# The MLP's second product as seven block products, with the token combinations made in its first

## The chip, the cores and the metric

The kernel runs on one core of a Trainium2 chip. A core has five engines that each work through a queue of their own, in order: TensorE (PE) multiplies, VectorE (DVE), ScalarE (ACT) and GpSimd (POOL) work element by element, and SyncE (SP) issues the transfers between memory and the core's SBUF. Products are added up in PSUM, which the other engines read. The metric is the time of one execution on the device in microseconds; a lower number is better. The kernel before takes 3046.49 us, the median of three runs (3045.34 to 3056.3). Everything runs in fp32, and a product in fp32 is made of three matmuls: each operand is split into a rounded part "hi" and a remainder "lo", and hi·hi, lo·hi and hi·lo are added.

## The reference

One decoder layer on 2048 tokens of width 1024: two kinds of attention, a cross-attention, and an MLP. The change touches the last step of the MLP and what the step before it leaves behind:

```python
    u = rms_norm(x, g_mlp[l]) @ w_up[l]
    x = x + jnp.square(jax.nn.relu(u)) @ w_down[l]
return rms_norm(x, g_final)
```

`w_up` is 1024 x 4096 and `w_down` 4096 x 1024.

## The kernel before

The tile framework orders the work when the kernel is built: its scheduler lays down one queue for each engine, with a wait at an instruction that needs another engine's result or a buffer that is still in use. At run time an engine goes through its queue in order. Buffers come from pools: 36 "main" tiles of 4 KB per partition, 6 "stage" tiles for what is loaded, smaller "work" tiles, and PSUM banks s (four), t (two) and o (two).

`phase_up` makes u = relu(x·w_up)². It takes the tokens in two halves of 1024, and in each half the 4096 columns in 16 pairs of 256. A pair is a 2 x 2 block matrix of weights times a 2 x 2 block matrix of tokens, and it uses seven block products in place of eight (Winograd's form): `product` (L1085 to L1097) splits one weight block or sum of blocks (ACT at L1088, POOL or DVE at L1089) and issues 84 matmuls in a pair. The sums of weights s1 to s4 are made on POOL (L1080 to L1083). The token combinations t1 to t4 stand ready in SBUF as operands: `mlp_combine` (L1009 to L1042) makes those of half 1 during pairs 4 to 11 of half 0 and puts them to memory, and `mlp_operands` (L1045 to L1067) loads and splits all seven when the halves change. `out` (L1102 to L1107) finishes one 128 x 512 block of u and stores it, four for each pair.

`phase_down` multiplies u by `w_down` directly. It goes over 16 slices of 256 rows of `w_down`. For a slice `slab` (L109 to L117) loads two weight tiles of 128 x 1024 and splits them (ACT at L116, POOL at L117), and for each of four chunks of 512 tokens a tile of u is loaded and split (ACT at L141, DVE at L142). Then eight output blocks of six matmuls each follow (L1179), each added by DVE into an accumulator in SBUF (L1183) that began as the residual x2: 3072 matmuls of 512 columns in all. `finish` (L1142 to L1171) makes the last norm of a chunk: squares on ACT (L1149), their sum on POOL or DVE (L1153), column sums on PE, the scale, and the store.

## Time and profile before

| | |
|---|---|
| median of three runs | 3046.49 us (3045.34 to 3056.3) |
| the profiled execution | 3047.63 us |
| its span in the trace | 3045.6 us, granted clock 0.974 of full speed |
| busy: PE / DVE / ACT / POOL | 95% / 58% / 37% / 38% |
| `phase_up` on PE | about 1665.7 to 2302.7 us |
| `phase_down` on PE | 2302.7 to 3006.4 us |
| after the last product | 39.2 us |

The profiled execution lies 1.1 us above the median, and 2.0 us of it are outside the span. "Busy" is the share of the span in which an engine executes; the chain of waits goes back from the last instruction to what released each step.

### The profile page before, as it was taken

How to read it: one execution, taken by the hardware profiler on the slowest of the kernel's cores; microseconds unless marked ns; L12 is line 12 of the kernel's file. 1: busy time of each engine (PE TensorE's matmuls, PEld its weight loads, DVE VectorE, ACT ScalarE, POOL GpSimd, SP SyncE). 2: the span in 40 equal slices, each digit the busy share in tenths (PEclk: the TensorE clock that was granted, in tenths of full speed). 3: DMA queues.
4: the chain of work that ended last, by engine and by line, in shares of the span. 5: the costliest groups of instructions: out<-in, count | busy, mean ns of one | idle time of the engine just before them, and what ended most of it. 6: DMA issues, size and time to landing. Idle time of an engine off the chain costs nothing.

```text
span 3045.6 us, 38727 instructions
## 1 busy us (share of the span) xinstructions
PE 2884.5 (95%) x13740; PEld 2350.0 (77%) x13740; DVE 1760.0 (58%) x2918; ACT 1125.9 (37%) x2481; POOL 1163.8 (38%) x914
## 2 busy tenths in 40 slices
PE   8999989989999899999995999989999999999996
PEld 8978866666666688888883877878888888888886
DVE  5254448887788642423345756665556566656656
ACT  7221137666767422444223333433342111111113
POOL 0133336765676542112124666665561101110115
PEclk9999989989999999999997999999999999999997
DMA  8443363434432664211327345443346122212203
GB/s 310 133 178 126 111 197 115 121 84 140 126 109 81 196 208 138 84 42 66 108 90 276 124 148 170 145 154 111 111 139 228 63 76 77 77 63 77 77 7 111
DMA packets 223297, 380.21 MB, mean 125 GB/s; under 512 B 25313, under 2 KB 95105, under 8 KB 223105
## 3 DMA queue, kind: packets, MB, share of 16 engines
q1 hardware_dynamic: 223104, 377.75, 37.5%
q8 instruction: 108, 1.77, 0.2%
q14 instruction: 85, 0.69, 0.1%
HBM read 259.65 MB, written 116.98 MB: 124 GB/s over the span
## 4 chain that ended last, share of the span: by engine, by line
PE 61%; DVE 5%; DMA 4%; POOL 4%; issue 2%; ACT 1%; SPq 0%; POOLq 0%; DVEq 0%; ACTq 0%
PE pd L1179 23%; PE p L1093 15%; PE po L804 6%; PE sc L868 6%; PE po L992 5%; PE sc L482 1%; DMA xs<-x_d 1%; DVE p L528 1%; PE o L543 1%; POOL w L1089 1%; PE wo L659 1%; DMA wf<-w_up 1%; PE pv L934 1%; PE pq L828 1%; POOL p L521 1%
## 5 line engine op out<-in xcount | busy, mean ns | idle before, releaser
L1093 PE MATMUL p<-xh,w 128*128 128x512 f32 x1792 | 557.3, 392 | 42.9 <-ACT w L1088 27.6
L1183 DVE TENSOR_TENSOR acc<-pd,acc 128x512 f32<-128x512 f32 (+1 forms) x520 | 351.2, 681 | 253.7 <-PE pd L1179 251.2
L1093 PEld LDWEIGHTS p<-xh,w 128*128 128x128 f32 x1792 | 337.0, 189 | 121.3 <-ACT w L1088 29.6
L1179 PE MATMUL pd<-uh,wdh 128*128 128x512 f32 (+1 forms) x1040 | 401.7, 386 | 1.0 <-DVE acc L1183 1.0
L1179 PE MATMUL pd<-ul,wdh 128*128 128x512 f32 (+1 forms) x1040 | 401.2, 386 | 0.0
L1179 PE MATMUL pd<-uh,wdl 128*128 128x512 f32 (+1 forms) x1040 | 401.2, 386 | 0.0
L1093 PE MATMUL p<-xl,w 128*128 128x512 f32 x896 | 350.3, 391 | 0.0
L117 POOL TENSOR_TENSOR wdl<-wf,wdh 128x1024 fp32r<-128x1024 f32 x32 | 78.0, 2440 | 549.6 <-ACT wdh L116 543.8
L489 ACT ACTIVATE p<-sc,nm 128x512 f32<-128x512 f32 (+3 forms) x320 | 198.8, 627 | 95.9 <-DVE nm L488 94.3
L482 PE MATMUL sc<-kt,q 128*128 128x512 f32 (+2 forms) x640 | 199.1, 414 | 32.0 <-ACT p L489 22.4
L1179 PEld LDWEIGHTS pd<-uh,wdh 128*128 128x128 f32 x1040 | 195.3, 188 | 40.4 <-DVE acc L1183 1.2
L1179 PEld LDWEIGHTS pd<-ul,wdh 128*128 128x128 f32 x1040 | 195.3, 188 | 39.4
L1179 PEld LDWEIGHTS pd<-uh,wdl 128*128 128x128 f32 x1040 | 195.3, 188 | 39.3
L488 DVE TENSOR_REDUCE nm<-sc 128x1 f32<-128x512 f32 (+3 forms) x320 | 184.3, 601 | 51.5 <-PE sc L487 29.4
L1093 PEld LDWEIGHTS p<-xl,w 128*128 128x128 f32 x896 | 169.1, 189 | 35.2
L482 PEld LDWEIGHTS sc<-kt,q 128*128 128x128 f32 x640 | 108.7, 199 | 84.4 <-ACT p L489 43.4
L521 POOL TENSOR_TENSOR p<-p,scl 128x512 f32<-128x512 f32 (+3 forms) x144 | 151.6, 1081 | 55.0 <-DVE scl L516 50.2
L141 ACT CAST uh<-uf 128x1024 fp32r<-128x1024 f32 x64 | 65.8, 1049 | 276.2 <-PE pd L1179 263.7
L303 PE MATMUL pa<-hh,wh 128*128 128x512 f32 x416 | 162.7, 391 | 0.0
L303 PE MATMUL pa<-hl,wh 128*128 128x512 f32 x416 | 162.5, 391 | 0.0
L303 PE MATMUL pa<-hh,wl 128*128 128x512 f32 x416 | 162.1, 390 | 0.0
L172 POOL TENSOR_TENSOR tot<-tot,sq 128x512 f32<-128x512 f32 x56 | 77.5, 1384 | 207.8 <-ACT sq L171 206.1
(266 smaller groups left out, 6051.8 us busy)
## 6 DMA issues: line engine op xcount, KB each, us to landing
wf<-w_up SPq DMA_DIRECT2D x64, 512.0 KB
u_d<-u SPq DMA_DIRECT2D x128, 256.0 KB
uf<-u_d SPq DMA_DIRECT2D x64, 512.0 KB
qk_d<-rot SPq DMA_DIRECT2D x96, 256.0 KB
x_d<-x SPq DMA_DIRECT2D x32, 512.0 KB
x<-x_d SPq DMA_DIRECT2D x32, 512.0 KB
xs<-x_d SPq DMA_DIRECT2D x32, 512.0 KB
wf<-w_down SPq DMA_DIRECT2D x32, 512.0 KB
```

What stands on the lines that cost most here:

```text
L117: getattr(nc, eng).tensor_tensor(lo, wf, f(hi), op=ALU.subtract)
L303: nc.tensor.matmul(pa, s_[d // 4][:, P * (d % 4) : P * (d % 4) + P], hs(m_, c, d), start=(d == 0 and i == 0), stop=(d == DT - 1 and i == 2),)
L482: mm = nc.tensor.matmul(sc[:, :um], q[:, x, c, P * t : P * t + P], kt[:, c, :um], start=(x == 0), stop=(x == 1 and not last))
L488: nc.vector.tensor_reduce(nm[:, t, j, c : c + 1], sc[:, :u], axis=AX.X, op=ALU.max, negate=True)
L489: nc.scalar.activation(p[:, c, :u], sc[:, :u], AF.Exp, bias=nm[:, t, j, c : c + 1], accum_out=l[:, t, j, c : c + 1])
L521: nc.gpsimd.tensor_tensor(p[:, 1, :u], p[:, 1, :u], sc[:, t, j, 1:2].broadcast_to([P, u]), op=ALU.mult)
L804: nc.tensor.matmul(po, wo[d][s_][:, P * n : P * n + P], m_[d // 2][:, d % 2], start=(d == 0 and z == 0), stop=(d == 7 and z == 2))
L868: nc.tensor.matmul(sc[n], x[s_][d][:, ts], wq[d][m_][:, 512 * n : 512 * n + 512], start=(d == 0 and z == 0), stop=(d == DT - 1 and z == 2))
L992: nc.tensor.matmul(po[i], vw[b][s_][:, P * n : P * n + P], m_[b], start=(b == 0 and z == 0), stop=(b == 7 and z == 2))
L1093: nc.tensor.matmul(ps, t[:, s_, P * d : P * d + P], x[d][m_], start=(d == 0 and z == 0), stop=(d == 3 and z == 2))
L1179: nc.tensor.matmul(pd, w[ft][s_][:, P * n : P * n + P], u[m_][:, ft, ts], start=(ft == 0 and z == 0), stop=(ft == 1 and z == 2))
L1183: nc.vector.tensor_tensor(av, pd, av, op=ALU.add)
```

## The change

The product with `w_down` takes the form of the first one. The loop is now over two halves of the tokens, four groups of 1024 rows of `w_down`, and seven products. A product has four output blocks (m) of 12 matmuls, so there are 2 x 4 x 7 x 4 x 12 = 2688 matmuls (the last product is done in two pieces of 256 columns). Seven accumulators of 512 x 512 take the place of the residual sums: in the first group of a half ACT copies the PSUM block into the accumulator (L1264), in the later ones DVE adds it (L1266). The accumulators are put together at the end of the half (`total`), and the residual is added on POOL. `weights` loads four blocks of `w_down` for a group into wide tiles, once for each half, and makes the sums in one tile `ws` on POOL and DVE (L1211). `parts` splits weights ("wd") and tokens ("ub") in two pieces of 128 x 1024 each: the cast on ACT (L1192), the lower part of the first piece on POOL and of the second on DVE (both L1193).

The token combinations are made in `phase_up`: each pair adds two subtractions on DVE and two on POOL and stores seven blocks in place of four.

```diff
-            nc.sync.dma_start(k.u_d[CHUNKS[2 * half + j]][n][i], u)
+            if (i, j) != (0, 1):
+                nc.sync.dma_start(k.u_d[half][f"b{i + 1}{j + 1}"][n], u)
+            return u
...
+        t = [k.main([P, 2, 512], F32, name="ut") for _ in range(2)]
+        t1, t2, t3, t4 = (x[:, i] for x in t for i in range(2))
+        nc.vector.tensor_tensor(t1, b12, b11, op=ALU.subtract)
+        nc.gpsimd.tensor_tensor(t2, b22, t1, op=ALU.subtract)
+        nc.gpsimd.tensor_tensor(t3, b22, b12, op=ALU.subtract)
+        nc.vector.tensor_tensor(t4, b21, t2, op=ALU.subtract)
+        for i, x in enumerate((t1, t2, t3, t4)):
+            nc.sync.dma_start(k.u_d[half][f"t{i + 1}"][n], x)
...
+    PRODUCTS = ((1, "b11"), (6, "t2"), (5, "t1"), (7, "t3"), (2, "b21"), (3, "b22"), (4, "t4"))
...
+    def parts(src, name):
+        res = []
+        for y in range(2):
+            x = src(y)
+            t = [k.main([P, 2, 512], name=name) for _ in range(2)]
+            nc.scalar.copy(t[0], x)
+            (nc.vector if y else nc.gpsimd).tensor_tensor(t[1], x, f(t[0]), op=ALU.subtract)
+            res.append(t)
+        return res
...
+        def combine(out, p, q, op):
+            for y, eng in enumerate((nc.gpsimd, nc.vector)):
+                ys = slice(2 * y, 2 * y + 2)
+                eng.tensor_tensor(out[:, ys], p[:, ys], q[:, ys], op=op)
+        yield parts(cut(a11), "wd")
+        s = wide("ws", "s", 1)
+        combine(s, a21, a22, ALU.add)
+        s1 = parts(cut(s), "wd")
+        combine(s, s, a11, ALU.subtract)
+        yield parts(cut(s), "wd")
+        yield s1
...
+                        if first:
+                            nc.scalar.copy(av, pd)
+                        else:
+                            nc.vector.tensor_tensor(av, pd, av, op=ALU.add)
...
+                if g == 3 and n == 3:
+                    ends.append(finish(acc[3] + acc[7], CHUNKS[2 * half + 1], 0, 512, False))
+                    step(-1)
```

ACT in the first group of the second product, after the change (copies of PSUM into accumulators, casts of the next product's weights "wd" and tokens "ub"):

```order
L1264 COPY acc_20394<-pd_20593 128x512
L1264 COPY acc_20394<-pd_20607 128x512
L1264 COPY acc_20395<-pd_20621 128x512
L1192 CAST wd_20651<-wa_20407 128x1024
L1192 CAST wd_20655<-wa_20407 128x1024
L1264 COPY acc_20395<-pd_20635 128x512
L1192 CAST ub_20661<-ub_20659 128x1024
L1192 CAST ub_20667<-ub_20665 128x1024
L1264 COPY acc_20396<-pd_20671 128x512
L1264 COPY acc_20396<-pd_20685 128x512
L1264 COPY acc_20397<-pd_20699 128x512
```

and the same engine early in `phase_down` before:

```order
L141 CAST uh_20556<-uf_20554 128x1024
L141 CAST uh_20626<-uf_20624 128x1024
L141 CAST uh_20696<-uf_20694 128x1024
L116 CAST wdh_20764<-wf_20766 128x1024
L116 CAST wdh_20770<-wf_20772 128x1024
L141 CAST uh_20778<-uf_20776 128x1024
L141 CAST uh_20848<-uf_20846 128x1024
```

Before, ACT had casts alone there; after, a product's fourth copy stands between the casts of the next product's weights and those of its tokens.

SP at the seam of the two products, after the change (the last pair's stores to `u_d`, then the first loads of `w_down`; "x2" at the end of a row stands for two such rows):

```order
L1108 DMA u_d1b11_110<-u_20330 128x512
L1129 DMA u_d1t1_113<-ut_20376 128x512
L1129 DMA u_d1t3_115<-ut_20377 128x512
L1129 DMA u_d1t2_114<-ut_20376 128x512
L1108 DMA u_d1b21_111<-u_20371 128x512
L1129 DMA u_d1t4_116<-ut_20377 128x512
L103 DMA wa_20404<-w_down 128x2x512 x2
L103 DMA wa_20407<-w_down 128x2x512 x2
L103 DMA wa_20410<-w_down 128x2x512 x2
L103 DMA wa_20413<-w_down 128x2x512 x2
```

and before, where SP took up `w_down` three pairs ahead of the end of `phase_up`:

```order
L1107 DMA u_d0_12_115<-u_19624 128x512
L1107 DMA u_d1_12_131<-u_19645 128x512
L1107 DMA u_d0_12_115<-u_19666 128x512
L1107 DMA u_d1_12_131<-u_19687 128x512
L103 DMA wf_20150<-w_down 128x1024
L103 DMA wf_20156<-w_down 128x1024
L103 DMA uf_20160<-u_d3_0_151 128x2x512
L1107 DMA u_d0_13_116<-u_19776 128x512
L1107 DMA u_d1_13_132<-u_19797 128x512
L103 DMA acc_20166<-x2_d3_174 128x2x512
```

The loads of `w_down` have moved behind the last store of `phase_up`.

ACT at the end of a half, around the last product t4 of the fourth group, after the change ("sq" are the squares of `finish`):

```order
L1192 CAST ub_22508<-ub_22506 128x1024
L1192 CAST ub_22514<-ub_22512 128x1024
L1192 CAST wd_22587<-wa_22069 128x1024
L1192 CAST wd_22591<-wa_22069 128x1024
L1162 ACTIVATE sq_22576<-acc_20400 128x1024
L1162 ACTIVATE sq_22578<-acc_20401 128x1024
L1162 ACTIVATE sq_22581<-acc_20396 128x1024
L1162 ACTIVATE sq_22584<-acc_20397 128x1024
L1192 CAST ub_22597<-ub_22595 128x1024
```

and at the first `finish` before:

```order
L141 CAST uh_24574<-uf_24572 128x1024
L141 CAST uh_24580<-uf_24578 128x1024
L141 CAST uh_24586<-uf_24584 128x1024
L141 CAST uh_24592<-uf_24590 128x1024
L1149 ACTIVATE sq_24660<-acc_20166 128x1024
L1149 ACTIVATE sq_24662<-acc_20168 128x1024
L1149 ACTIVATE sq_24665<-acc_20170 128x1024
L1149 ACTIVATE sq_24668<-acc_20172 128x1024
```

Before, all casts stood ahead of the squares; after, the four squares stand ahead of the cast of t4's tokens.

## Rows read from the trace of the kernel before

**Rows 1.** The page's busy time by engine, and its chain of waits by line.
```profile
PE 2884.5 (95%) x13740; PEld 2350.0 (77%) x13740; DVE 1760.0 (58%) x2918; ACT 1125.9 (37%) x2481; POOL 1163.8 (38%) x914
...
PE pd L1179 23%; PE p L1093 15%; PE po L804 6%; PE sc L868 6%; PE po L992 5%; PE sc L482 1%; DMA xs<-x_d 1%; DVE p L528 1%; PE o L543 1%; POOL w L1089 1%; PE wo L659 1%; DMA wf<-w_up 1%; PE pv L934 1%; PE pq L828 1%; POOL p L521 1%
```

**Rows 2.** Busy time by stretch: start:end, length, engines, clock, DMA, GB/s.
```profile
1640.70:1665.70 25.00, 1.14 (x2) 0.00 (x0) 17.38 (x17) 16.94 (x21) 9.94 (x4) 0.50 1.00 364
1730.00:1885.00 155.00, 147.44 (x635) 118.17 (x635) 91.53 (x122) 55.49 (x98) 94.01 (x65) 1.00 0.49 165
1985.80:1997.30 11.50, 1.03 (x4) 0.33 (x3) 11.50 (x11) 5.29 (x8) 8.46 (x5) 0.68 0.90 319
2130.00:2230.00 100.00, 100.00 (x443) 82.81 (x442) 50.96 (x74) 37.85 (x64) 60.54 (x44) 1.00 0.31 109
2302.70:2312.70 10.00, 10.00 (x46) 8.28 (x45) 8.29 (x12) 3.14 (x4) 2.79 (x1) 1.00 1.05 387
2402.00:2602.00 200.00, 200.00 (x884) 165.62 (x883) 123.21 (x165) 26.56 (x26) 21.70 (x9) 1.00 0.22 69
3006.40:3045.60 39.20, 14.76 (x67) 13.88 (x65) 19.07 (x51) 12.60 (x24) 17.41 (x17) 0.55 0.35 124
```

**Rows 3.** Lines by shape, 2302 to 3000: count, busy, mean ns, idle before.
```profile
L1183 DVE TENSOR_TENSOR acc<-pd,acc 128x512 f32<-128x512 f32 x504 | 344.7, 690 | 251.7 <-PE pd L1179 249.5
...
L142 DVE TENSOR_TENSOR ul<-uf,uh 128x1024 fp32r<-128x1024 f32 x60 | 80.7, 1364 | 6.1 <-ACT uh L141 6.1
L117 POOL TENSOR_TENSOR wdl<-wf,wdh 128x1024 fp32r<-128x1024 f32 x30 | 72.7, 2426 | 547.9 <-ACT wdh L116 542.1 <-PE p L1093 5.8
L141 ACT CAST uh<-uf 128x1024 fp32r<-128x1024 f32 x60 | 61.6, 1049 | 272.4 <-PE pd L1179 263.7 <-issue 8.7
...
L1153 POOL TENSOR_TENSOR sq<-sq 128x1024 f32<-128x1024 f32 x7 | 16.8, 2400 | 62.3 <-ACT sq L1149 62.3
L1149 ACT ACTIVATE sq<-acc 128x1024 f32<-128x1024 f32 x10 | 10.6, 1062 | 39.2 <-DVE acc L1183 29.4 <-PE col L181 4.3 <-DVE rs_t L160 2.6
```

**Rows 4.** Lines by shape, 1665 to 2302.
```profile
L1089 POOL TENSOR_TENSOR w<-s,w 128x512 fp32r<-128x512 f32 x64 | 100.5, 1571 | 126.8 <-ACT w L1088 119.4 <-DVE u L1100 3.6 <-DMA wf<-w_down 1.8
...
L1082 POOL TENSOR_TENSOR s<-wf 128x512 f32<-128x512 f32 x32 | 51.0, 1594 | 18.4 <-DVE w L1089 17.8 <-DVE rs_t L161 0.6
...
L1110 ACT COPY c<-p 128x512 f32<-128x512 f32 x32 | 18.6, 580 | 11.8 <-PE p L1093 11.8
```

**Rows 5.** Waits of TensorE from 1665 to 2303: total, times, longest.
```profile
PE p L1093 <- ACT w L1088: 27.6, 2, 23.9
PE p L1093 <- DVE w L1089: 11.2, 4, 6.7
```

**Rows 6.** The chain of waits, 1736 to 1765: start, duration, what.
```profile
1739.06 3.85 DMA xs<-x_d
...
1745.43 5.79 DMA wf<-w_up
...
1751.37 1.30 POOL s L1080
...
1759.93 3.67 DMA xs<-x_d
```

**Rows 7.** Timeline of TensorE at 1665 and 1990: start, duration, [idle before].
```profile
1665.72 0.80 PE L1093 MATMUL p<-xh,w 128*128 128x512 f32 x1 [23.88 <-ACT w L1088]
...
1989.56 0.55 PE L1093 MATMUL p<-xh,w 128*128 128x512 f32 x1 [3.75 <-ACT w L1088]
...
1997.27 1.22 PE L1093 MATMUL p<-xh,w 128*128 128x512 f32 x2 [6.73 <-DVE w L1089]
```

**Rows 8.** Line 117: duration ns min/median/max, first and last start.
```profile
L117 POOL TENSOR_TENSOR wdl<-wf,wdh x32: 2392/2412/2897, 2255.9 to 2912.7; 128x1024 fp32r<-128x1024 f32 x32
```

**Rows 9.** The chain of waits at the end, 2960 to 3046.
```profile
3007.86 2.36 POOL sq L1153
...
3021.05 1.28 POOL o L1167
```

More of the change, by code (lines that the diff above doesn't have):

```diff
@@ L1115, in pair @@
         mid()
-        out(1, 1, add(p7, w, "u"))
-        out(0, 0, add(product(a12, "b21", "s", "gpsimd"), c1, "u"))
-        out(0, 1, add(product(s4, "b22", "t", "vector"), w, "u"))
-        out(1, 0, add(product(a22, "t4", "s", "gpsimd"), z, "u"))
+        b22 = out(1, 1, add(p7, w, "u"))
+        b11 = out(0, 0, add(product(a12, "b21", "s", "gpsimd"), c1, "u"))
+        b12 = out(0, 1, add(product(s4, "b22", "t", "vector"), w, "u"))
+        b21 = out(1, 0, add(product(a22, "t4", "s", "gpsimd"), z, "u"))
+        t = [k.main([P, 2, 512], F32, name="ut") for _ in range(2)]
[6 more added lines that the diff above has]
+            nc.sync.dma_start(k.u_d[half][f"t{i + 1}"][n], x)
     combine = mlp_combine(k, 1)
@@ L1169, in finish @@
                     nc.vector.scalar_tensor_tensor(o[:, i], av, g, row, op0=ALU.mult, op1=ALU.mult)
-            out_piece(o, CHUNKS[c], y, lo, w)
+            out_piece(o, ch, y, lo, w)
         yield
-    def lower(u, w, c, lo, wd, steps):
-        ts = slice(lo, lo + wd)
-        for n in range(DT):
-            pd = k.ps("s", [P, wd], name="pd")
-            for ft in range(2):
-                for z, (s_, m_) in enumerate(((0, 0), (1, 0), (0, 1))):
-                    nc.tensor.matmul(
-                        pd, w[ft][s_][:, P * n : P * n + P], u[m_][:, ft, ts], start=(ft == 0 and z == 0), stop=(ft == 1 and z == 2)
-                    )
-            av = acc[n // 2, c][:, n % 2, ts]
-            nc.vector.tensor_tensor(av, pd, av, op=ALU.add)
-            if n in steps:
-                next(steps[n])
@@ new lines, in parts, with weights @@
+    def parts(src, name):
[7 more added lines that the diff above has]
+        return res
+    def weights(g):
+        block = {}
+        for i, x in ((0, 0), (1, 0), (1, 1), (0, 1)):
+            block[i, x] = wide("wa", "a", 4)
+            for y in range(2):
+                ys = slice(4 * g + 2 * y, 4 * g + 2 * y + 2)
+                k.load(block[i, x][:, 2 * y : 2 * y + 2], w_down[x][:, ys, 512 * i : 512 * i + 512], chain="weights")
+        a11, a12, a21, a22 = (block[i, x] for i in range(2) for x in range(2))
+        cut = lambda t: lambda y: t[:, 2 * y : 2 * y + 2]
+        def combine(out, p, q, op):
[9 more added lines that the diff above has]
+        yield s1
+        combine(a21, a11, a21, ALU.subtract)
+        yield parts(cut(a21), "wd")
+        yield parts(cut(a12), "wd")
+        combine(s, a12, s, ALU.subtract)
+        yield parts(cut(s), "wd")
+        yield parts(cut(a22), "wd")
@@ L1217, in phase_down @@
     for x in (-1, -2, -1):
-        next(ends[x])
+        step(x)
 def build(nc, tc, a, out):
@@ L1237, in build @@
         k.t_d = [{n: dram(f"t_d{i}{n}", 2, 2, P, 512) for n in ("t1", "t2", "t3", "t4")} for i in range(2)]
-        k.u_d = [[dram(f"u_d{c}_{n}", 2, P, 512) for n in range(16)] for c in range(4)]
+        names = ("b11", "b21", "b22", "t1", "t2", "t3", "t4")
+        k.u_d = [{n: dram(f"u_d{i}{n}", 16, P, 512) for n in names} for i in range(2)]
         k.x1_d, k.x2_d = ([dram(f"{n}{c}", DT, P, 512) for c in range(4)] for n in ("x1_d", "x2_d"))
```

137 lines of the change are left out of this document (89 added, 48 removed).

## The prediction

> **What bounds the kernel now.** I read the page's busy times first, then the chain of waits, then the stretches of the MLP, and last the lines of `phase_down` by shape. TensorE is busy for 95% of the span and leads the chain; the product of `phase_down` (L1179) alone is 23% of the chain, that of `phase_up` (L1093) 15% [rows 1]. In the middle of `phase_down`, from 2402 to 2602 us, PE is busy for 200.00 of 200 us at full clock and starts 884 matmuls: 226.2 ns for each one of 512 columns. DVE is busy for 123 us there, ACT for 27 and POOL for 22 [rows 2]. So fewer matmuls are worth 226 ns each there, as long as the other engines keep their operands ready. There is no pause at the seam of the two products either: from 2302.7 PE is busy for 10.00 of 10 us, with the DMA at 387 GB/s [rows 2]. PE does wait in three places that the change touches: 7.6 us in 1730 to 1885, where half 1's combinations are made; around 1990, where the halves of `phase_up` change; and in the last 39.2 us [rows 2].
>
> **A. Matmuls.** 3072 become 2688: 384 x 0.2262 = **-86.8**. The number of PSUM blocks to evict falls from 520 to 224.
>
> **B. phase_up's new work.** A pair adds two subtractions on POOL, two on DVE and three stores. In most pairs there is room: POOL is busy for 60.5 and DVE for 51 of 100 us, and a pair lasts 84 x 0.2257 = 19.0 us [rows 2]; two POOL operations of 1.3 to 1.6 us [rows 4, 6] make POOL some 76%. Cost nothing, with that idle time as cover. In pairs 4 to 11 of half 0 the chain runs not through PE but through transfers and POOL: a load of x2 (3.85 us), one of w_up (5.79), then POOL's sums (1.30 the first), and the next load of x2 20.9 us after the last [rows 6]. POOL's t2 and t3 stand in that chain, and SP, which issues in order, has the stores of t2 and t4 ahead of the next loads. All eight pairs with two operations of 1.5 us and the stores' delay would give 28; nothing at all if they fall in the transfers' time. Three in five of the 24 us of POOL work: **+15** [0 to 28].
>
> **C. The change of halves in phase_up.** Before, operands of half 1 were cast while pair 15 ran; PE still waited 3.75 and 6.73 us [rows 7], about 11 with the little between; but for the start these are the longest waits of the phase [rows 5]. The new "ut" tiles take the main tiles that were free for this, and in the new order the first cast of an operand comes on ACT after pair 15's squares, so all 14 operands are made after pair 15. The nearest row is the start at 1665.72, with nothing ready: 23.88 us of waiting [rows 7]. I take 20 in place of 11: **+9** [4 to 14].
>
> **D. The seam of the products.** SP's first load of w_down now stands behind the last store of t4 (second pair of orders above). After the last matmul of `phase_up` come four element-wise steps of 0.6 to 0.7 us (0.58 and 0.69 in [rows 3, 4]), with their handovers 3.0; then the load, 5.8 like that of w_up [rows 6]; then the cast (1.05) and POOL's lower part (2.43) [rows 3]: 12.3. On top I put 3 us for matmuls at the lower clock, since after waits rows of 0.55 to 0.80 us stand where 0.39 is usual [rows 7]. **+15** [10 to 22], where there was no pause.
>
> **E. The first group of each half.** Here ACT evicts, and by the order its fourth copy stands between the next product's casts of weights and of tokens. So at each product's end PE waits for the copy (0.58), the cast (1.05) and POOL's lower part (2.43) [rows 3, 4], 4.06, with the drain of the last matmul and four handovers about 4.8; against it the scheduler lets 8 matmuls go ahead that need no lower part of the tokens, 1.8. That is 3.0 us, at t3, b21, t4 and at b11 of the next group. At b22 POOL has a sum of the next group's weights (2.4) ahead: 5.3. At t2 four POOL operations stand in a row behind the cast of s1 (lower parts of s1, s2 and of the tokens, the sum s2): 1.05 + 3 x 2.43 + 2.40 - 1.8 = 8.9. With 0.5 at t1 and 1 for the clock: 12 + 5.3 + 8.9 + 1.5 = 27.7 in a half, **+55** in both. If the engines had worked ahead it would be 0; if each wait is as long as the longest here, 8.9, it would be some 110. I stay with the sum of rows. In groups 1 to 3 the casts stand a whole product ahead, and DVE evicts: 4 x 0.69 + 2 x 1.36 (lower parts) + at most 2.6 (sums) = 8 us of DVE in a product of 48 x 0.226 = 10.9; POOL two lower parts and at most one sum, 7.3; ACT four casts, 4.2 [rows 3]. All fit: 0.
>
> The Trainium skill, "SBUF — State Buffer", section "SBUF: two separate sides", says that a DVE operation with two SBUF inputs and a GpSimd operation share a port pair as an exclusive lock, so that one blocks fully while the other runs. The trace agrees in kind: POOL's lower part takes 2392 ns at the least and 2897 at the most [rows 8].
>
> **F. The last product, t4, of both halves.** ACT has the four squares of the other chunk's `finish` ahead of the tokens' cast (third order), and POOL two sums ahead of the lower part. The last addition of b22 and its total 2, two squares 2.1, two POOL sums 4.8, the lower part 2.4, less 1.8 of matmuls: 9.3 each, with [rows 3]; **+18.6** [8 to 25].
>
> **G. Start of half 1 of phase_down.** The second chunk's squares and sums delay the first tokens by 7.5 (three POOL sums of 2.4 in the way [rows 3]); column and row matmuls that move in between take 2.6; POOL's residuals in the last group 3. **+13** [6 to 20].
>
> **H. The tail.** Before, after the last product two chunks were still to be finished, in the chain from 3007.86 to 3021.05 the one before the last [rows 9]. Now it is one chunk, whose first 256 columns are done ahead. 13.2 us go: **-13** [-20 to 0].
>
> **Sum.** -86.8 + 15 + 9 + 15 + 55 + 18.6 + 13 - 13 = +26. The profiled execution has 3047.6, 1.1 above the median of 3046.5, so I forecast 3046.5 + 26 = 3072.5, say **3073**.
>
> **Rivals.**
> R1, faster: the engines prepare ahead in the first groups too. For it: ACT has 4 x 1.05 + 4 x 0.58 = 6.5 us of work in a product of 10.9 [rows 3, 4], and it is idle for most of `phase_down` now. Against it: the order itself, where the token casts stand behind the fourth copy. E is gone then: 3073 - 55 = 3018.
> R2, about the same: B and C cost nothing, since POOL and DVE had time and the operand transfers come out as late as before. For it: PE waits only 7.6 us in the 155 of the combinations [rows 2]. 3073 - 24 = 3049.
> R3, slower still: every wait makes the clock fall. For it: after a wait of 3.75 us a matmul is listed with 0.55 us, after 6.73 with two in 1.22 [rows 7], and the granted clock of that stretch is 0.68 [rows 2]. Fourteen waits in the first groups at 2 us each add 28: 3101.
> R4, slower: DVE's and POOL's work on two SBUF operands excludes each other, so each of 14 restarts is longer by one lower part on DVE, 1.36 [rows 3]: +19, 3092. That is what the page named above would make of it. Against it: the longest POOL row is only 0.5 us above the median [rows 8].
>
> **How the numbers follow.** The forecast has 0.50, with a range of its own from 3058 to 3090; R1 0.12, R2 0.20, R3 0.12, R4 0.06. A measurement of this kernel can tell about 0.5%, 15 us, from no change: 3031 to 3062. Faster is R1, 0.12; within is R2, 0.20; slower is the rest, 0.68. The range that leaves out 2 in 10 goes from 3036 to 3108: it leaves out R1 and a little beyond R3.
>
> **What would show it.** In the profile after, `phase_down` has 224 blocks of 12 matmuls, at a cadence of 226 ns in groups 1 to 3 with PE at 100% (A). In the first group of each half PE shows six pauses, of 3 us most and of 9 at t2, which ACT's cast or POOL's lower part at L1192 and L1193 ends (E); two of 9 us ahead of t4 in the fourth groups (F); 12 us at the seam, ended by a cast of wd or its lower part (D); 20 us in place of 11 at the change of halves (C); more than 7.6 us of waits in pairs 4 to 11 (B); and an end of about 26 us after the last matmul of the product (H). It is wrong if PE is busy throughout the first groups (R1), if pauses come in groups 1 to 3, or if the clock in the first groups lies well under 1 (R3).

## The result and the profile after

The changed kernel takes **3125.88 us**, the median of four runs (3121.96 to 3127.49), against 3045.91 before: 1.0254 times as long, with a 95% interval of 1.0228 to 1.0279. The forecast was 3073, with 3108 as the upper end. The direction was right, the size was not: 80 us more in place of 26. The profiled execution has 3126.88 us and a span of 3124.7.

Where the time went, by the first and the last matmul of each product in the two traces (us):

| stretch | before | after | change | forecast |
|---|---|---|---|---|
| start to first matmul of `phase_up` | 1665.7 | 1668.5 | +2.8 | 0 |
| `phase_up` | 637.0 | 671.2 | +34.2 | +24 (B, C) |
| seam of the products | 0 | 12.2 | +12.2 | +15 (D) |
| `phase_down` | 703.7 | 746.3 | +42.6 | 0 (A, E, F, G) |
| last matmul of the product to the end | 39.2 | 26.5 | -12.7 | -13 (H) |

The sum is 79.1, the difference of the spans. In other kernels below whose code is the same up to `phase_up`, its first matmul starts anywhere between 1661.7 and 1673.5, so the first line tells nothing.

The busy line of the page after (engine, us, share of the span, instructions), to be set beside [rows 1]:

```profile
PE 2836.7 (91%) x13356; PEld 2292.3 (73%) x13356; DVE 1970.7 (63%) x2744; ACT 1274.9 (41%) x2665; POOL 1683.3 (54%) x1106
```

384 matmuls have gone, worth 87 us at 226 ns each, but PE's busy time is only 48 us less, 2836.7: the other matmuls are busy for longer. Its share has fallen from 95% to 91%, and GpSimd has gone from 1163.8 us to 1683.3.

The same stretches as in [rows 2], with their places in the kernel after (start:end, length, busy time of PE, PEld, DVE, ACT, POOL, granted clock, DMA share, GB/s):

```profile
1730.00:1885.00 155.00, 136.95 (x574) 106.87 (x573) 116.80 (x128) 49.35 (x87) 111.41 (x73) 0.99 0.54 184
2010.00:2030.00 20.00, 0.00 (x0) 0.00 (x0) 18.26 (x15) 12.15 (x15) 9.12 (x3) 0.51 0.82 282
2130.00:2230.00 100.00, 100.00 (x443) 82.84 (x442) 70.04 (x84) 37.47 (x65) 78.18 (x54) 1.00 0.42 150
2339.70:2351.90 12.20, 0.23 (x2) 0.00 (x0) 3.65 (x5) 3.72 (x5) 5.43 (x3) 0.72 0.80 285
2351.90:2485.50 133.60, 104.40 (x409) 79.66 (x409) 79.21 (x31) 53.93 (x68) 78.75 (x28) 0.92 0.36 122
2463.80:2467.80 4.00, 3.68 (x9) 2.53 (x10) 4.00 (x2) 3.10 (x4) 3.98 (x3) 0.59 0.00 0
2485.50:2645.00 159.50, 158.32 (x697) 130.78 (x697) 132.85 (x100) 57.79 (x59) 129.88 (x42) 1.00 0.49 165
2717.20:2754.00 36.80, 21.40 (x95) 18.51 (x95) 22.05 (x34) 13.97 (x19) 19.34 (x10) 0.73 0.49 161
3098.00:3124.70 26.70, 8.69 (x51) 8.07 (x49) 15.81 (x39) 7.55 (x16) 11.61 (x13) 0.59 0.45 158
```

Read PE's busy time against the length, and then the clock. A steady stretch of `phase_up` (2130) is as it was, full, though POOL now has 78 us of 100 and DVE 70: the new work is hidden there, as B said. The pairs with half 1's combinations (1730) leave PE idle for 18 us in place of 7.6. From 2010 to 2030, at the change of halves, there is no matmul at all. The stretch of the first group of `phase_down` (2351.9, with the first products of the next group) has PE idle for 29 of 134 us at a mean clock of 0.92, whereas the rest of group 1, group 2 and the start of group 3 (2485.5) are as good as full. In the stretch from 2717.2, where half 1 of `phase_down` begins, the clock is 0.73.

`phase_up` cut by its matmuls, pairs 0 to 3 and then pairs 4 to 11 of half 0, the first two rows before and the last two after:

```profile
1665.72:1746.95 81.23, 79.74 (x337) 64.65 (x337) 56.38 (x65) 27.66 (x48) 58.12 (x38) 0.96 0.35 123
1746.95:1909.49 162.54, 155.45 (x673) 125.28 (x672) 95.32 (x128) 60.11 (x105) 99.41 (x69) 1.00 0.48 162
1668.48:1756.08 87.60, 80.80 (x336) 64.61 (x337) 66.12 (x71) 28.28 (x49) 69.35 (x45) 0.96 0.41 146
1756.08:1929.39 173.31, 158.47 (x674) 125.92 (x672) 130.34 (x144) 59.00 (x104) 126.66 (x84) 0.99 0.54 186
```

Pairs 0 to 3 have become 6.4 us longer, though the forecast gave them no cost, and pairs 4 to 11 10.8. Pairs 12 to 15 are as long as before (75.9), the pause at the change of halves is 21.5 longer and half 1 is 4.5 shorter: 34.2 in all.

Lines of `phase_down` by shape, to be set beside [rows 3] (count, busy us, mean ns, idle before):

```profile
L1193 POOL TENSOR_TENSOR ub<-ub 128x1024 fp32r<-128x1024 f32 x56 | 185.5, 3314 | 6.5 <-ACT ub L1192 6.4
L1193 DVE TENSOR_TENSOR ub<-ub 128x1024 fp32r<-128x1024 f32 x56 | 135.8, 2427 | 40.2 <-ACT ub L1192 36.7 <-DMA out<-o 2.6 <-POOL ub L1193 0.9
...
L1193 POOL TENSOR_TENSOR wd<-wa,wd 128x1024 fp32r<-128x1024 f32 x32 | 92.4, 2888 | 99.9 <-ACT wd L1192 93.1 <-DMA wa<-w_down 6.8
L1193 DVE TENSOR_TENSOR wd<-wa,wd 128x1024 fp32r<-128x1024 f32 x32 | 85.6, 2675 | 82.9 <-ACT wd L1192 82.6
...
L1211 POOL TENSOR_TENSOR ws<-wa 128x1024 f32<-128x1024 f32 x8 | 27.1, 3383 | 2.4 <-DVE wd L1193 2.4
```

The forecast was added up without these durations. A lower part of 128x1024 was 2426 ns on POOL and 1364 on DVE before; for the tokens it is 3314 and 2427 now. A sum of two weight blocks, which I had put at 2400, takes 3383.

PE in the first group of half 0, which had no like in the kernel before (start, us, matmuls, idle time before and what ended it):

```profile
2351.90 12.83 PE L1255 MATMUL pd<-ub,wd 128*128 128x512 f32 x48 [11.97 <-ACT ub L1192]
2372.91 3.40 PE L1255 MATMUL pd<-ub,wd 128*128 128x512 f32 x8 [8.18 <-ACT ub L1192]
...
2399.79 2.14 PE L1255 MATMUL pd<-ub,wd 128*128 128x512 f32 x8 [1.73 <-ACT ub L1192]
2403.17 9.37 PE L1255 MATMUL pd<-ub,wd 128*128 128x512 f32 x40 [1.24 <-POOL ub L1193]
...
2428.74 2.14 PE L1255 MATMUL pd<-ub,wd 128*128 128x512 f32 x8 [1.73 <-ACT ub L1192]
2436.68 11.18 PE L1255 MATMUL pd<-ub,wd 128*128 128x512 f32 x40 [5.80 <-POOL ub L1193]
...
2464.12 12.92 PE L1255 MATMUL pd<-ub,wd 128*128 128x512 f32 x48 [1.79 <-ACT ub L1192]
```

From t3 on each product starts 1.73 us late, at the cast of its tokens on ACT, gets through 8 matmuls and stops again for 1.24 us until POOL has their lower part: 2.97 us, at three of the products. At b22 the second stop is 5.80 us, since POOL makes a sum first, and the two are 7.5. That is the pattern of E, with 3.0 and 5.3 forecast. Some rows are also slow: 8 matmuls take 3.40 us in place of 2.14 after the pause of 8.18, and 40 take 11.18 in place of 9.37 after that of 5.80.

And the two other places, at the change of halves in `phase_up` and at t4 and its norm in `phase_down`:

```profile
2030.97 0.79 PE L1093 MATMUL p<-xh,w 128*128 128x512 f32 x1 [25.26 <-ACT w L1088]
...
2702.46 3.78 PE L1255 MATMUL pd<-ub,wd 128*128 128x512 f32 x8 [8.75 <-ACT ub L1192]
...
2726.99 2.07 PE L197 MATMUL row<-ident,rs 128*128 128x128 f32 x8 [8.13 <-DVE rs L162]
```

The 25.26 us stand where before there were 3.75 and 6.73 [rows 7]. In the last of these rows PE waits for the scale of a norm, with the next product's matmuls queued behind.

### The profile page after: what moved, and what is told of

Same layout as the page of the kernel before. It is cut to its first block, busy times and chain, and to the rows that moved or that the text cites. A ratio compares the mean times of both kernels' runs of the same rounds, so it can differ in the third digit from the quotient of the medians.

```text
span 3124.7 us, 38213 instructions
## 1 busy us (share of the span) xinstructions
PE 2836.7 (91%) x13356; PEld 2292.3 (73%) x13356; DVE 1970.7 (63%) x2744; ACT 1274.9 (41%) x2665; POOL 1683.3 (54%) x1106
## 5 line engine op out<-in xcount | busy, mean ns | idle before, releaser
L1255 PE MATMUL pd<-ub,wd 128*128 128x512 f32 (+1 forms) x2736 | 645.1, 397 | 96.2 <-ACT ub L1192 63.0
L1255 PEld LDWEIGHTS pd<-ub,wd 128*128 128x128 f32 x2736 | 519.8, 194 | 220.2 <-ACT ub L1192 70.5
L1192 ACT CAST ub<-ub 128x1024 fp32r<-128x1024 f32 x112 | 114.6, 1050 | 201.1 <-issue 87.4
L1193 POOL TENSOR_TENSOR ub<-ub 128x1024 fp32r<-128x1024 f32 x56 | 185.5, 3314 | 6.5 <-ACT ub L1192 6.4
L1106 ACT ACTIVATE u<-u 128x512 f32<-128x512 f32 x128 | 81.0, 633 | 242.3 <-DVE u L1105 242.3
L1193 DVE TENSOR_TENSOR ub<-ub 128x1024 fp32r<-128x1024 f32 x56 | 135.8, 2427 | 40.2 <-ACT ub L1192 36.7
L1193 POOL TENSOR_TENSOR wd<-wa,wd 128x1024 fp32r<-128x1024 f32 x32 | 92.4, 2888 | 99.9 <-ACT wd L1192 93.1
L868 PE MATMUL sc<-wq,xh 128*128 128x512 f32 x512 | 144.9, 395 | 0.0
L1089 POOL TENSOR_TENSOR w<-s,w 128x512 fp32r<-128x512 f32 x64 | 101.1, 1580 | 72.0 <-ACT w L1088 72.0
```

The source lines that it names most:

```text
L868: nc.tensor.matmul(sc[n], x[s_][d][:, ts], wq[d][m_][:, 512 * n : 512 * n + 512], start=(d == 0 and z == 0), stop=(d == DT - 1 and z == 2))
L1089: getattr(nc, eng).tensor_tensor(t[:, 1], w, f(t[:, 0]), op=ALU.subtract)
L1106: nc.scalar.activation(u, u, AF.Square)
L1192: nc.scalar.copy(t[0], x)
L1193: (nc.vector if y else nc.gpsimd).tensor_tensor(t[1], x, f(t[0]), op=ALU.subtract)
L1255: nc.tensor.matmul(pd, wd[kk // 2][s_][:, kk % 2, P * m : P * m + P], ub[kk // 2][m_][:, kk % 2, ts], start=(kk == 0 and z == 0), stop=(kk ...
```

## The experiments

All single times are to be read with what repeats show: the kernel after lay between 3122 and 3127.5 us, the kernel before between 3042 and 3056. Each run of an edited kernel had runs of the kernel before beside it on the same chip. Phase lengths are from each kernel's own trace.

**What each half of the change costs by itself.** In the kernel before, only the four subtractions and their stores were added to `phase_up`:

```diff
+        nc.vector.tensor_tensor(t1, b12, b11, op=ALU.subtract)
+        nc.gpsimd.tensor_tensor(t2, b22, t1, op=ALU.subtract)
...
+            nc.sync.dma_start(k.ut_d[half][f"t{i + 1}"][n], x)
```

Expected: 

> The kernel before, with the four subtractions and their four stores added to each pair of phase_up (eight stores in all; phase_down does not read them). If phase_up's new work costs what the trace of after shows, by itself, phase_up is 32 to 38 us longer, and the whole is 3078 to 3092 with a few us at the seam. If only my estimate of 24 is due to it and the rest to other parts of the change, it is 3068 to 3074.

Measured: 3085.29 us, 40.6 more than the 3044.69 beside it. `phase_up` is 669 us long, 32 more than before; behind it the seam has 3.5 us and the old `phase_down` takes 710.6, 7 more. Waits of PE from 1905 to 2350 us (total, times, longest):

```profile
PE p L1093 <- ACT w L1088: 23.2, 1, 23.2
PE pd L1188 <- ACT uh L141: 3.5, 1, 3.5
PE pd L1188 <- DVE ul L142: 1.8, 1, 1.8
```

The wait of 23.2 us at the change of halves is there, and small ones at the seam. So the new work costs 32 us in `phase_up` by itself, as expected, and some 10 more behind it.

The other half: `phase_up` as before, `phase_down` as after, reading b-blocks where it would read t1 to t4.

```diff
-                    k.load(t, k.u_d[half][name][lo : lo + 2]...)
+                    k.load(t, k.u_d[half][{"t1": "b12", "t2": "b22", "t3": "b12", "t4": "b21"}.get(name, name)][lo : lo + 2]...)
```

Expected: 

> The changed phase_down with phase_up as before: four stores for each pair and no combinations. phase_down reads b12, b22, b12 and b21 where it would read t1 to t4, so the products are taken of the wrong token blocks; the work and its sizes in phase_down are those of the change. If the costs of the two phases add up (the run with the combinations alone in the kernel before took 40.6 us more than before), this takes 3126 - 40 = 3082 to 3090. If phase_up's stores and tiles also hold up the start of phase_down, it is less, 3070 to 3080; if phase_down's pauses only grow with nothing to wait for at the seam, more.

Measured: 3089.9 us, 41 more than the 3048.55 beside it; `phase_down` 748 us long, the seam 10.1. The totals add up: 41 + 41 = 82, and the change measured 80. By phases the new work is 32 us in `phase_up` alone and 34 in the change, and `phase_down` is 44 longer alone and 43 in the change; the 10 us that the first of these runs lost behind `phase_up` are not in the change, so the nearness of the totals is in part luck. What is wrong with the forecast can be looked for in each phase apart.

This run also bears on the seam (D): without the stores of t1 to t4 the loads of `w_down` still stand behind the last store. In the change their tiles come from a pool ("down") that is made after `phase_up`'s pool ("work") has been closed. That this is why they wait is inferred; no run changes it.

**The order on ScalarE in the first groups (E).**

```diff
-                            nc.scalar.copy(av, pd)
+                            nc.vector.tensor_copy(av, pd)
```

Expected: 

> The kernel after, with the first group's evictions as copies on VectorE in place of ScalarE, so that no copy stands ahead of a cast. If the order of copies and casts on ScalarE makes the pauses (theory O), the pauses of 3 us in the first groups go, the 7.5 at b22 shrinks, and the clock there comes back to 1: phase_down gets shorter by 45 to 75 us, the whole 3050 to 3080. If VectorE and GpSimd, whose lower parts take 2.4 and 3.3 us there in place of 1.4 and 2.4, are what the products wait for (theory L), the pauses stay and are put down to them: 3110 or more.

Measured: 3084.75 us, some 41 less than the change; `phase_down` 709 us in place of 746. PE in the first group, from the second product on:

```profile
2367.67 27.52 PE L1255 MATMUL pd<-ub,wd 128*128 128x512 f32 x109 [7.12 <-ACT ub L1192]
2396.40 0.49 PE L1255 MATMUL pd<-ub,wd 128*128 128x512 f32 x1 [1.21 <-DVE wd L1193]
2397.53 32.43 PE L1255 MATMUL pd<-ub,wd 128*128 128x512 f32 x138 [0.64 <-DVE ub L1193]
2431.09 1.66 PE L1255 MATMUL pd<-ub,wd 128*128 128x512 f32 x6 [1.13 <-POOL ub L1193]
2435.47 64.81 PE L1255 MATMUL pd<-ub,wd 128*128 128x512 f32 x276 [2.72 <-DVE ub L1193]
```

Products now run on: 109 and 138 matmuls without a stop. The pauses that are left are other ones, of t2 and of lower parts on both engines. So the copy ahead of the casts is the cause of half of E's cost: of 77 us (below) 39 are gone from the first groups and their next products, 37 from `phase_down` as a whole. Of the 45 that I had at the least, 8 did not come, and the whole lies 5 over the range that I gave it. (The copies could go to VectorE: the section on the chip says that "the other engines" read PSUM, but in these traces only VectorE and ScalarE do, and no GpSimd instruction has a PSUM tile as input.)

**Two engines that slow each other (R4).** All lower parts on DVE:

```diff
-            (nc.vector if y else nc.gpsimd).tensor_tensor(t[1], x, f(t[0]), op=ALU.subtract)
+            nc.vector.tensor_tensor(t[1], x, f(t[0]), op=ALU.subtract)
```

Expected: 

> The kernel after, with all lower parts of phase_down on VectorE and none on GpSimd, which keeps half of the sums of weights, the residuals and the norms. Theory L: VectorE and GpSimd shut each other out, so that a lower part takes 2.4 to 2.7 us on VectorE in place of 1.4; then it takes 1.2 to 1.4 us here, the pauses of 1.2 and 5.8 us that GpSimd's lower part ends go, and the whole is 15 to 30 us shorter: 3096 to 3111. If VectorE is then the engine that the products wait for (four lower parts, four additions and half of the sums in 10.9 us), pauses come in groups 1 to 3 as well, and the whole is the same or longer.

Measured: 3095.68 us, 30 less than the change; `phase_down` 718 us. The lines on DVE by shape (mean ns after the bar):

```profile
L1193 DVE TENSOR_TENSOR ub<-ub 128x1024 fp32r<-128x1024 f32 x112 | 176.5, 1589 | 47.7 <-ACT ub L1192 47.7
...
L1193 DVE TENSOR_TENSOR wd<-wa,wd 128x1024 fp32r<-128x1024 f32 x64 | 80.2, 1277 | 72.7 <-ACT wd L1192 72.6
...
L1211 DVE TENSOR_TENSOR ws<-ws,wa 128x1024 f32<-128x1024 f32 x8 | 24.4, 3047 | 0.1
...
L1211 DVE TENSOR_TENSOR wa<-wa 128x1024 f32<-128x1024 f32 x8 | 11.8, 1470 | 0.0
```

The same instruction as in the lines after above, on the same engine, falls from 2427 ns to 1589 for the tokens and from 2675 to 1277 for the weights, once POOL has no lower parts to make. One sum of weights still takes 3047 on average, POOL making its half beside all eight of them; another takes 1470, with POOL beside one of the eight. So the two engines do hold each other up, and the pauses that POOL's lower part ended are gone. The kernel after shows how, where sums and lower parts follow each other on both engines:

```profile
2504.98 3.38 POOL L1193 TENSOR_TENSOR ub<-ub 128x1024 fp32r<-128x1024 f32 x1
2506.63 2.82 DVE L1211 TENSOR_TENSOR ws<-wa 128x1024 f32<-128x1024 f32 x1
2508.32 3.38 POOL L1211 TENSOR_TENSOR ws<-wa 128x1024 f32<-128x1024 f32 x1
2509.48 3.30 DVE L1211 TENSOR_TENSOR wa<-wa 128x1024 f32<-128x1024 f32 x1
```

DVE's row begins while POOL's runs and ends 1.09 us after it (2509.45 and 2508.36); POOL's next begins while DVE's runs and ends 2.25 after that; and DVE's next ends 1.08 after POOL's. In `phase_down` all 142 DVE rows of this size and kind (two inputs in SBUF) that begin while one of POOL's runs end 1.08 to 1.17 us after it, however early they began, and all 130 of POOL's that begin while one of DVE's runs end 2.20 to 2.28 after it. Alone such a row takes 1.21 to 1.23 us on DVE and 2.34 to 2.41 on POOL. So the one that comes second stands still until the first is done, and its listed time contains that wait. The Trainium skill, "SBUF — State Buffer", section "SBUF: two separate sides", has it as an exclusive lock; the trace agrees, with these numbers.

The 30 us are not the price of this alone. A lower part that meets nothing is also 1.1 us shorter on DVE than on POOL, and it no longer queues behind POOL's sums; the run does not separate the three. Of the 28 us by which `phase_down` is shorter, 17 lie in the first groups and their next ones and 11 in the fourth.

Both edits together, with the weight sums on POOL alone:

```diff
+                            nc.vector.tensor_copy(av, pd)
+            nc.vector.tensor_tensor(t[1], x, f(t[0]), op=ALU.subtract)
+            for y, eng in enumerate((nc.gpsimd, nc.gpsimd)):
```

Expected: 

> The kernel after, with the first group's evictions and all lower parts on VectorE and the sums of weights on GpSimd alone. The two edits gave 41 and 30 us by themselves. If they remove different pauses (the copy ahead of the casts, and the two engines shutting each other out), they add up in part: 3060 to 3078. If both only shorten the same pauses, 3078 to 3088. If VectorE, with 4 x 0.7 + 4 x 1.3 = 8 us of 10.9 in a product, becomes the bound, over 3090.

Measured: 3091.96 us, `phase_down` 708.6, as long as with the first edit alone. Nothing adds up: both shorten the same pauses, and waits for DVE's lower parts take their place (20.3 us in all, 17 times). The move of the sums, a third edit, was not tried by itself. Single runs of 3085 and 3092 are too near each other to rank them.

**The clock (R3).** Extra matmuls whose result nobody reads, to keep PE busy in the pauses of the first groups:

```diff
+                fill = {1: 36, 6: 8, 5: 8, 7: 8, 2: 24, 3: 8, 4: 8}[n] if first else 0
+                        nc.tensor.matmul(pd, wd[1][0][:, 1, 0:P], ub[1][0][:, 1, 0:512], ...)
```

Expected: 

> The kernel after, with 100 extra matmuls in the first group of each half (36 after the first product, 24 after b21, 8 after the others) into a spare PSUM bank that nothing reads, to keep TensorE busy in the pauses. They do not shorten what the products wait for. If about 9 us in each first group are a clock that falls after a pause (theory K), the granted clock there rises from 0.92 to about 1 and the whole gets shorter by 10 to 20 us, to 3105 to 3115. If the slower matmuls after a pause are a price of the restart itself, the whole stays at 3122 to 3130 or gets longer by the extra matmuls' overhang.

Measured: 3144.26 us, 18 more. The scheduler put most of them behind the first 8 matmuls of the next product, so that the pause of 1.73 us ahead of these stayed and the product was put off. It settles nothing on the clock. The next try filled the long pauses alone:

```diff
+            if n == 15 and name == "t4":
+                count = 100 if half == 0 else 46
...
+                count_ = {(0, 1): 32, (3, 3): 34}.get((g, n), 0)
```

Expected: 

> The kernel after, with extra matmuls that nothing reads in the long pauses of TensorE alone: 100 at the change of halves of phase_up, 46 at the seam of the products, 16 in and 16 behind the first product of each half and 34 ahead of the last product t4 of each half. They fill most of the pauses of 25, 12, 8 and 9 us, without shortening what the products wait for. Theory K: the clock falls in these pauses, and the matmuls behind each run at half speed for some 4 us; then the first 48 matmuls of phase_down take 11.1 us in place of 12.8, those behind the other pauses come back likewise, and the whole is 8 to 15 us shorter: 3110 to 3118. Theory R: the slow stretch is a price of starting again that the extra matmuls only move ahead, so that it is paid in the pause; the trace then shows a slow stretch in the extra matmuls, and the time falls all the same. If neither holds, the first product still takes 12.8 us and the whole 3122 or more.

Measured: 3139.93 us, 14 more, so both sizes were wrong. At the seam the extra matmuls read a tile of `phase_up`'s pool, which the loads of `w_down` seem to wait for, and the first product starts 18.5 us after the last of `phase_up` in place of 12.4. That part is spoiled. The change of halves is clean:

```profile
2001.45 22.83 PE L1100 MATMUL fill<-xh,w 128*128 128x512 f32 x100
2024.77 0.50 PE L1093 MATMUL p<-xh,w 128*128 128x512 f32 x1 [0.49 <-ACT w L1088]
...
2026.92 0.73 PE L1093 MATMUL p<-xh,w 128*128 128x512 f32 x2 [1.42 <-DVE w L1089]
...
2032.46 0.73 PE L1093 MATMUL p<-xh,w 128*128 128x512 f32 x2 [1.12 <-DVE w L1089]
```

100 extra matmuls at the full rate, with a granted clock of 1.00, fill the pause, and the first real matmul behind it is listed with 0.50 us in place of 0.79. Still it is 309.0 us from there to the end of `phase_up`'s last matmul, as it was: 309.0 after, and 309.0 to 309.5 in five other kernels with the same code there. Behind the pause PE now waits in small steps for the first pair's split weights, 3.1 us in three steps; in the kernel after, at half clock, it reached them later and waited 0.90. At this pause, then, the lower clock cost nothing that could be won back; elsewhere that stays open.

**The change of halves (C).** The combinations in four small work tiles in place of two main tiles:

```diff
-        t = [k.main([P, 2, 512], F32, name="ut") for _ in range(2)]
-        t1, t2, t3, t4 = (x[:, i] for x in t for i in range(2))
+        t1, t2, t3, t4 = (k.w2(name="ut") for _ in range(4))
```

Expected: 

> The kernel after, with the token combinations of phase_up in four small work tiles, so that the six main tiles are free for the operands of half 1 as before. If the taken main tiles cause the longer wait at the change of halves (theory M), the wait falls from 26 to about 11 us and some 3 us of clock come back: 3105 to 3113. If the seven stores in the queue of SyncE ahead of the operands' loads cause it (theory S), the wait stays at 24 or more: 3120 to 3130.

Measured: 3121.14 us, 5 less than the change, most of it ahead of `phase_up`. PE at the change of halves:

```profile
2016.18 0.79 PE L1093 MATMUL p<-xh,w 128*128 128x512 f32 x1 [7.29 <-ACT w L1088]
...
2021.34 1.22 PE L1093 MATMUL p<-xh,w 128*128 128x512 f32 x2 [3.94 <-DVE w L1089]
```

7.29 + 3.94 in place of 25.26 + 0.90: theory M holds for the wait itself, and main tiles are its cause. In the 65 us around it PE starts 195 matmuls in place of 158, which is worth 8 us. But `phase_up` is 669.5 us, less than 2 shorter: the pairs of half 0 take 10 us longer than in the kernel after and half 1 takes 6 longer. There are eight small tiles of this kind, and a pair now takes ten (w, z, four of u and four of ut), which may be why. The wait was moved, not removed.

**The pairs with half 1's combinations (B).** t2 and t3 on VectorE:

```diff
-        nc.gpsimd.tensor_tensor(t2, b22, t1, op=ALU.subtract)
-        nc.gpsimd.tensor_tensor(t3, b22, b12, op=ALU.subtract)
+        nc.vector.tensor_tensor(t2, b22, t1, op=ALU.subtract)
+        nc.vector.tensor_tensor(t3, b22, b12, op=ALU.subtract)
```

Expected: 

> The kernel after, with the combinations t2 and t3 of phase_up on VectorE in place of GpSimd. If GpSimd's two subtractions in the chain of transfers and weight sums make the 13 us of new waiting in pairs 4 to 11 of half 0 (theory P), that waiting falls to 8 to 12 us in all, near the 7.6 of before, and the whole to 3110 to 3118. If the stores ahead of the loads in the queue of SyncE make it (theory S), it stays within 4 us and so does the whole, 3120 to 3130.

Measured: 3120.47 us, `phase_up` 666.0; PE waits 16.9 us from 1670 to 1905 us in place of 21.6. That says little, since the run of the norm below, with `phase_up`'s code untouched, has 16.1. Pairs 4 to 11 say more: 168.2 us, where the kernel after has 173.3 and six others with the same code 171.6 to 174.1. So some 5 us are gone from these pairs, 3 of them clear of that spread; it lies between the two theories. The stores out of SyncE's queue:

```diff
-            nc.sync.dma_start(k.u_d[half][f"t{i + 1}"][n], x)
+            nc.scalar.dma_start(k.u_d[half][f"t{i + 1}"][n], x)
```

Expected: 

> The kernel after, with the stores of t1 to t4 issued by ScalarE in place of SyncE. Theory S (stores ahead of loads in SyncE's queue): the waiting in pairs 4 to 11 of half 0 falls from 21.6 us, the first waits of the phase included, to 12 or less, and the whole by 10 to 15, to 3111 to 3116. Theory P (GpSimd's subtractions): the waiting stays at 18 or more and the whole at 3119 to 3130, or more where ScalarE's casts now stand behind a store that waits.

Measured: 3125.66 us. Waits of PE from 1670 to 1905 us:

```profile
PE p L1093 <- POOL w L1089: 10.8, 9, 2.3
PE p L1093 <- DVE v L1100: 4.7, 4, 2.3
PE p L1093 <- ACT w L1088: 4.1, 3, 2.1
```

With the 1.6 us on DVE's weights 21.2 in all, as before the edit, and the seam is not shorter either (12.0). So theory S's gain did not come. It is not refuted outright: the waits on POOL fell from 13.3 to 10.8 us and those on ACT, which now issues the stores ahead of its casts, rose from 1.0 to 4.1. GpSimd's subtractions make a part of B, some 5 us; of the rest the cause stays open.

**The norm at the end of a half (F, G).**

```diff
                 wd, ub = next(w), parts(tokens, "ub")
+                if g == 3 and n == 4:
+                    ends.append(finish(acc[3] + acc[7], CHUNKS[2 * half + 1], 0, 512, False))
+                    step(-1)
```

Expected: 

> The kernel after, with the squares of the other chunk's norm written behind the operands of the last product t4 in place of ahead of them, in both halves. If the four squares on ScalarE and the two sums on GpSimd ahead of t4's tokens make the pauses of 10.3 and 9.5 us (theory O), these pauses go, and with them some 2 us of clock behind each: 3126 less 20 to 24, so 3100 to 3107, if the end is not longer for it. If something else ends them (a stage buffer, the residuals on GpSimd), the pauses stay within 3 us of that and the whole is 3118 or more.

Measured: 3119.46 us. The pauses ahead of t4 are gone, and `phase_down` is 730.5 us, 16 shorter; but the end after it is 40.3 us in place of 26.5, since the norm now comes later. In `phase_down` others came:

```profile
2712.07 3.58 PE L181 MATMUL col<-ones,sq 128*128 128x1 f32 x16 [11.13 <-POOL sq L1166]
...
2748.24 2.05 PE L197 MATMUL row<-ident,rs 128*128 128x128 f32 x8 [16.38 <-DVE rs L162]
```

The column sums and the scale of a norm stand in PE's queue where they were put, and the products behind them wait with them. Theory O holds for the cause of the pauses and was wrong on the gain.

**Better versions.** Three small tiles, t1 in place of b12, and t1, t2 and t4 on VectorE, on top of the run with all lower parts there:

```diff
+        t2, t3, t4 = (k.w2(name="ut") for _ in range(3))
+        t1 = b12
```

Expected: 

> The same as the run before it in this list, and in phase_up three small work tiles in place of two main tiles (t1 made in place of b12), with three of the four subtractions on VectorE. Small tiles alone took the wait at the change of halves from 26 to 11 us and gave back 10 elsewhere, since eight such tiles were too few; the subtractions on VectorE gave 5. If the tiles were the cause of that, three in place of four leave 10 to 15 us: 10 to 20 less than the run before it in this list. If GpSimd's chain is what is late, less than 8.

Measured: 3076.99 us, 15 less than without; `phase_up` 655.7 us in place of 672.6. Whether the tile less or the subtractions on VectorE did it was not told apart. Then the combinations made in `phase_down`, and `phase_up` left as before:

```diff
+                    if name == "t2":
+                        kept[y] = less(block(y, "b12"), block(y, "b11"))
+                        t = less(block(y, "b22"), kept[y])
...
+                    if name == "t4":
+                        return less(block(y, "b21"), block(y, "t2"))
```

Expected: 

> phase_up as before, with four stores; the token combinations are made in phase_down on GpSimd from the loaded blocks (8 subtractions of 128x1024 for each group, some 23 us of GpSimd in a group of 76; t2 is stored and loaded once more for t4), with evictions and lower parts on VectorE as in the two runs before. If phase_up's 40 us are the price of making the combinations there, and GpSimd has the room in phase_down, the whole is the run of those edits less 30 to 40: 3020 to 3050, at or below the kernel before. If GpSimd is late with them (two subtractions behind loads for t2, ahead of the second product), pauses of 5 to 10 us come at t2 in every group, 8 of them, and the whole stays over 3060.

Measured: 3117.34 us (four runs; 1.0219 times the kernel before, 1.0199 to 1.0239). `phase_up` is back at 635.9 us, but `phase_down` has 769. PE at the end of half 0:

```profile
2663.66 8.22 PE L1266 MATMUL pd<-ub,wd 128*128 128x512 f32 x24 [4.33 <-DVE acc L1277]
2685.07 3.78 PE L1266 MATMUL pd<-ub,wd 128*128 128x512 f32 x8 [13.19 <-ACT ub L1183]
```

Eight subtractions for a group crowd DVE as well as POOL: DVE's lower parts of tokens are back at 1.9 us, waits of 3 to 4 us for its additions come in the last groups, and the pause at t4 is 13 us. Against the run with both edits (3091.96), 37 us were saved in `phase_up` and 60 spent in `phase_down`.

Last, what gave most, together: the first group's copies on VectorE and the three small tiles, with t1, t2 and t4 on VectorE.

Expected: 

> The kernel after, with the first group's evictions on VectorE (41 us less by itself), t1 to t4 in three small tiles and t1, t2 and t4 on VectorE (15 us less in the run with all lower parts on VectorE). If the pauses in the two phases are independent, as the two halves of the change were (41 and 43 us, 79 together), this takes 3126 - 41 - 15 = 3070, within 5. It stays slower than the kernel before by 20 to 30 us, since the change of halves, the seam and the last products still wait.

Measured: 3073.76 us, as added up (four runs; 1.0082 times the kernel before, 1.0065 to 1.0099). Faster than the change by 52, and still slower than the kernel before.

## Why the prediction went wrong

- **A** held: the cadence from 2485.5 to 2645 us is 159.5 us for 697 matmuls, 229 ns with the small waits. But pauses did come in groups 1 to 3, where A and E had none: 0.26 to 0.85 us in the second product of group 1, and in the fourth groups 1.34 us at t1 in each half and 3.34 at b22 in half 0. (The blocks to evict are 228, with the last product's pieces counted as in the 520.)
- **E is the step that failed**, by its size, and it failed most in what it gave the matmuls around the pauses. The pauses stand where it put them, and the run with the copies on VectorE shows that their order makes half of the cost. Taken as length less matmuls at 226 ns, half 0's first group and the next two products lost 41.1 us (133.6 - 409 x 0.2262), of which 2.0 in the slow first product belong to D, and half 1's 38.3 (98.2 - 297 x 0.2262, and 7.3 ahead of it). In parts, for both halves:

| E | forecast | measured |
|---|---|---|
| pauses of PE | 53 | 58 |
| matmuls around the pauses, beyond 226 ns each | 2 | 19 |
| sum | 55 | 77 |

Of the 19, some 11 are matmuls at half clock: an estimate, half of the time that PE is busy there in stretches of granted clock 0.50. Some 5 more are an estimate too: before each of 28 stops the last matmul takes its full 0.39 us and not the 0.226 of the cadence. The rest is not assigned.

- E's pauses came out near the sum partly by luck. At t3, b21 and t4 POOL's lower part took 3.30 us in place of 2.43, but what E had added for drain and handovers, 0.7, did not come: ahead of t3 the fourth copy begins at 2398.21, the cast at 2398.68 and POOL at 2399.82, so copy and cast take 1.6 us together. At t2 the pauses are 9.0 in half 0 for 8.9. At b22, where POOL's sum takes 3.38 and the lower part 3.32, nothing made up for it: 7.5 for 5.3. (E's own terms add up to 5.4 there, and F's to 9.5, not 9.3.)
- **R4** had the mechanism of these longer rows, and I gave it 6 in 100 on a wrong reading. I looked at POOL's rows alone [rows 8]. DVE's lower parts in the same trace (nanoseconds at the least, median and most) show it:

```profile
L142 DVE TENSOR_TENSOR ul<-uf,uh x64: 1207/1226/1808, 2265.6 to 2935.0; 128x1024 fp32r<-128x1024 f32 x64
```

In `phase_down` before, 14 of them, of 1.75 to 1.81 us, began while POOL's lower part ran, and each ended 1.08 us after it. The 1364 ns that I used is a mean of these and of rows that met nothing. R4's price was wrong too: in E's pauses it shows at b22 alone, some 2 us in each half.

- **R3** fell as it was put, since not every pause made the clock fall: the granted clock is 1.00 from 2398 to 2433 us, through three pauses of 1.73 us and two of 1.24. But after one of 1.79 us, at the head of group 1, it did fall (0.59 from 2463.8 to 2467.8), and a price like R3's 28 us came, over the whole phase and not in the first groups alone: in `phase_down` after, PE is busy for 53.4 us in stretches of granted clock 0.50. Half of this, some 27 us, is an estimate of the most that the clock can have cost; before, no such stretch lies between 2302.7 and 3006.4 us. The sum had 5 for it, 3 at the seam and 2 in E.
- **F and G**: F measured 10.3 and 9.5 us of waiting for 9.3 each. For G 13 was forecast; from 2693.7 to 2754 us alone the losses beyond F and t2's wait are some 21 us. I had counted the column and row matmuls by their own time, not that PE's queue stands still until the scale is ready (8.13 us). With the smaller pauses named above all that `phase_down` lost outside D and E is some 50 us more than before, for 32.
- **C**: the cause of the wait was right (the main tiles), the size not: 26.2 us of waiting in place of 20. My bound of 14 more than before was broken by 2, since I had taken "nothing ready" at 23.9 us as an end that could not be reached.
- **B** came out at 17 us for 15, but by luck: pairs 4 to 11, which were meant, are 10.8 us longer, and pairs 0 to 3, which had been given nothing, 6.4. The cause is known for some 5.
- **D** came out at 12.2, with 2.0 in the slow first product, for 15. Its steps up to the first load took 4.3 us for 3.0 and the load 4.2 for 5.8, two errors that cancel. **H** came out at -12.7 for -13.
- **R1** and **R2** did not come; in half 0's pairs 0 to 11 and at the change of halves nothing of the new work was hidden.

Of the 53 us by which the forecast was short, 22 are E, 18 the fourth groups and the start of half 1, 8 C, 2 B and 3 the start of `phase_up`, which tells nothing. But for D, the errors have one sign. Each term was a sum of undisturbed steps, and the upper end of the range held too little for what several late engines do to each other and for what a pause costs beyond its own length.

## What to carry to other kernels

A product saved on TensorE is worth its time only if the engines that feed it keep ahead; look in the built order for the first place where an eviction stands ahead of the next operands' casts. Give a pause of TensorE a price beyond its length: here 58 us of pauses in the first groups came with 19 us of slower matmuls and run ends. Take durations for a phase in which two engines will work side by side from rows where they already do: here they grew by 0.9 to 1.1 us each, and the spread of one row before (1207 to 1808 ns) had shown it. A wait that is removed by giving its buffer or its place to something else mostly comes back a few lines on; count both places.

## What was not expected of the hardware

A 128x1024 operation with two inputs in SBUF took 1.21 to 1.23 us on VectorE when GpSimd had no such operation running, and when it began beside one of GpSimd's it ended 1.08 to 1.17 us after that one, whenever it began; listed, it took up to 3.43 us. The wait stands in the row's own duration, not as idle time before it. 100 matmuls that kept TensorE's clock at its upper level of 2.4 GHz (granted 1.00) through a pause of 23 us did not shorten the phase by what the trace can tell: 309.0 us from there to its end, with and without them.
